# Mixture of experts on one core: the second expert's rows are transposed two blocks later, the rows' keys computed on VectorE, multiplications one stage later

## The chip, the cores and the metric

The kernel runs on one core of one Trainium2 chip. The metric is the device time of one execution in microseconds; the lower it is, the better. PE is TensorE, DVE VectorE, ACT ScalarE, POOL GpSimd and SP SyncE, whose queue issues the weight loads.

## What is computed

Two layers on 256 tokens of 1024 numbers in float32: a gated delta rule with a dense feed-forward, then attention in a window with a mixture of 8 experts, of which each token takes 2. The change is in the mixture alone:

```python
def swiglu(x, w_gate, w_up, w_down):
    return (jax.nn.silu(x @ w_gate) * (x @ w_up)) @ w_down

def moe_swiglu(x, w_router, w_gate, w_up, w_down):
    ...
    logits = (xf @ w_router).astype(jnp.float32)
    top_val, top_idx = lax.top_k(logits, TOP_K)          # TOP_K = 2
    top_w = jax.nn.softmax(top_val, axis=-1)
    gates = jnp.einsum('nk,nke->ne', top_w, jax.nn.one_hot(top_idx, N_EXPERTS, dtype=jnp.float32))
    out = jnp.zeros_like(xf)
    for e in range(N_EXPERTS):                           # 8
        h = jax.nn.silu(xf @ w_gate[e]) * (xf @ w_up[e]) # 1024 -> 3584
        out = out + gates[:, e:e + 1].astype(xf.dtype) * (h @ w_down[e])
    return out.reshape(bsz, t, d)
```

## The kernel before, in words

The mixture takes the time from about 470 us to the end. Its weights come as 336 loads of 1 MB on SP's queue into a ring of 10 buffers (`unit`, L140). Each loaded unit is split into a high and a low half: ScalarE casts `hi` (L154), VectorE subtracts to get `lo` (L155), into 4 pairs of buffers. Products of full precision are built from those halves: `mm3` (L167) takes high by high, low by high and high by low, 24 matmuls for one unit pair; a lighter form (`mm2`, L1192) packs the high and low half of up to 64 rows into one operand and takes 16. A branch on PE (`arms`, L1174) picks the form by the expert's number of rows. Expert 0 has no branch and takes the first form.

An expert's 3584 hidden numbers are 7 blocks of 512, worked through as pairs (0,1), (2,3), (4,5) and (6). The list `stages` (L1286) fixes the order of one pair: gate of both blocks, up of both blocks, the down projections of the pair before, and then "held", where the products of silu(gate) and up are multiplied (`V.tensor_mul`, L1355). The products are transposed on PE one stage later (`turn_one`, `turned`, L1240: transposes L1243, `hT` cast on ScalarE L1246, its low half on VectorE L1247). A stage is the order in the code; the scheduler sets the final order on each engine, and `issue_after` holds instructions back until the instruction that it names.

The tokens of expert 0 are picked by a one-hot matmul (L1127). Those of the other experts go through memory. `places` (L1064) works out, for each token and each of its two choices, the row in the buffer `xs`, on GpSimd with VectorE's sums between, and the two gate values `gat2`; the rows' keys become integers in `keyi` (L1079). Four scatters on GpSimd's queue (L1168, `xs<-x,keyi`) write the tokens there, each behind the landing of the one before. `fetch(e + 1)` (L1117) reads an expert's 128 rows back as `xr`, also on GpSimd's queue. `gather(e + 1)` (L1121) transposes them on PE (8 transposes, L1139), and ScalarE (L1141) and VectorE (L1142) make the halves `xg` of them, and the packed form `xp`. In the code, `fetch` is called at the up block 1 and `gather` at the up block 3 of the expert before.

Of the kernel before, what the change touches and what calls it, by code (L numbers as in the profile page):

```python
# [23 lines left out]
F32 = mybir.dt.float32  # L24
# [3 lines left out]
OP = mybir.AluOpType  # L28
AX = mybir.AxisListType

P = 128
# [7 lines left out]
E = 8  # L39
NE = 8  # L40
# [42 lines left out]
def kernel(ctx: ExitStack, tc: tile.TileContext, A, out):  # L83
# [83 lines left out]
    def mm3(ps, xh, xl, whs, first, last):  # L167
        n = len(whs)
        for k, (wh, _) in enumerate(whs):
            PE.matmul(ps, xh(k), wh, start=first and k == 0, stop=False)  # L170
            PE.matmul(ps, xl(k), wh, start=False, stop=False)  # L171
        for k, (_, wl) in enumerate(whs):
            PE.matmul(ps, xh(k), wl, start=False, stop=last and k == n - 1)  # L173
# [391 lines left out]
    p = trb()  # L565
# [498 lines left out]
    def places():  # L1064

        sq = [P, 2, E]
        row, spill, one, val = (rt.tile(sq, F32, name=n) for n in ("row", "spill", "one", "val"))
        G.tensor_tensor(row, pos, place[:, None, :E].to_broadcast(sq), op=OP.add)
        G.tensor_tensor(spill, place[:, E:, None].to_broadcast(sq), row, op=OP.subtract)
        G.tensor_scalar(val, pos, float(P), None, op0=OP.is_ge)  # L1070
        G.tensor_tensor(spill, spill, val, op=OP.mult)
        G.tensor_tensor(row, row, spill, op=OP.add)
        key = rt.tile([P, 2, 2], F32, name="key")
        for j in range(2):
            G.tensor_scalar(one, rank, float(j), None, op0=OP.is_equal)
            for src, dst in ((row, key), (gate, gat2)):
                G.tensor_tensor(val, one, src, op=OP.mult)
                V.tensor_reduce(dst[:, j], val, axis=AX.X, op=OP.add)
        V.tensor_copy(keyi, key)  # L1079
# [4 lines left out]
    with ExitStack() as mctx:  # L1084
# [36 lines left out]
        def gather(e):  # L1121
# [7 lines left out]

            if e == 0:  # L1130
                for k in range(KC):
                    pick(k, 0)
            for g in range(2):
                p = pg[g] if e == 0 else trb()
                for k in range(4 * g, 4 * g + 4):
                    if e == 0:
                        pick(k, 1)
                    else:
                        PE.transpose(p[:, k % 4 * P:(k % 4 + 1) * P], xr[e][:, k * P:(k + 1) * P], ident)  # L1139
                hi, lo = (xg[:, n, 4 * g:4 * g + 4, :].rearrange("p a c -> p (a c)") for n in range(2))  # L1140
                S.copy(hi, p)  # L1141
                V.tensor_sub(lo, p, hi.bitcast(F32))  # L1142
                if e:
                    packed(xp[e][:, 512 * g:512 * (g + 1)], p, lo)
# [17 lines left out]
        with tc.issue_after(placed.ins):  # L1162
            for tb in range(2):
                gates(tb, lgs[tb])
            places()
# [3 lines left out]
        for tb in range(2):  # L1169
            nc.gpsimd.dma_start(x3d[tb * P:(tb + 1) * P], x[tb])  # L1170
        NB = EF // 512
# [144 lines left out]

        for what, e, b in stages:
# [7 lines left out]
            if what == "gate":  # L1325
# [3 lines left out]
                if held:  # L1329
                    turn_one()  # L1330
# [5 lines left out]
            elif what == "up":  # L1336
# [5 lines left out]
                if whole:  # L1342
                    for n, (pg, pu) in enumerate(zip(pgs, pus)):
                        s_ = mp.tile([P, 512], F32, name="msg", tag="msg")
                        S.activation(s_, pg, AF.Silu)
                        mine.append((b - len(pgs) + 1 + n, pu, low(pu) if e else None, s_))
                if b == 1 and e + 1 < NE:
                    fetch(e + 1)
                if b == 3 and e + 1 < NE:
                    xg[e + 1] = gather(e + 1)  # L1350
            elif what == "held":
                if e:
                    arms(e, lambda: None, lambda: [addlow(pu, lu_) for _, pu, lu_, _ in mine])
                for bb, pu, _, s_ in mine:
                    V.tensor_mul(s_, s_, pu)  # L1355
                    held.append((e, bb, s_))
                mine.clear()
# [130 lines left out]
```

## Time and profile before

| | us |
| --- | --- |
| median of 3 runs | 1424.33 (1423.22 to 1425.75) |
| profiled execution | 1427.08 |
| its span, first to last instruction | 1425.4 |
| PE busy | 1314.1 |
| VectorE busy | 1165.6 |
| ScalarE busy | 1012.1 |
| GpSimd busy | 68.0 |

Busy times are shares of one execution that passes through stages with different limits, so they don't tell what bounds a given stage. An engine's timeline lists its instructions in order of their start; the difference between two starts is what one instruction takes of the engine, while the duration printed for a matmul holds the end of its pipeline as well. In brackets stands how long the engine was idle ahead of the instruction, and which event ended that.

### The profile page before, as it was taken

To read this page: it belongs to the slowest core of one execution; us is meant where nothing else is said; L and a number is where in the kernel's file an instruction comes from. 1 tells how busy PE (TensorE), PEld (TensorE's weight loads), DVE (VectorE), ACT (ScalarE), POOL (GpSimd) and SP (SyncE) were. 2 spreads that over 40 slices of the span, in tenths; PEclk is the share of its full clock that TensorE was granted. 3 is DMA by queue.
4 is the path that set the end of the run, shared out by engine and by line. 5 is a ranking of instruction groups with operands and counts; after the bars stand their busy time and mean duration, and the time that the engine had idled before them with its cause. 6 is when DMAs were issued, how large, how long until landed. Compare 5 with 4: busy or idle time off the path is not lost. (4 is left out here: it accounts for less than half of the span.)

```text
span 1425.4 us, 17392 instructions
## 1 busy us (share of the span) xinstructions
PE 1314.1 (92%) x6175; PEld 1046.2 (73%) x6175; DVE 1165.6 (82%) x1293; ACT 1012.1 (71%) x1264; POOL 68.0 (5%) x97
## 2 busy tenths in 40 slices
PE   7999999999898969988899999999889999888884
PEld 5888788888777858866677777776667777666663
DVE  4885975554878768889998887889999888999998
ACT  4764544443364657689888878779988888998983
POOL 4000000000000310000000000000000000002110
PEclk9999999999999889999999999999999999999997
DMA  8641577653644899999999999999999999999992
GB/s 283 208 125 60 178 271 237 229 207 120 226 148 170 307 366 336 362 368 392 419 413 380 367 358 368 376 343 408 413 420 411 377 369 374 396 414 416 419 416 87
DMA packets 145378, 446.76 MB, mean 313 GB/s; under 512 B 12704, under 2 KB 20032, under 8 KB 145264
## 3 DMA queue, kind: packets, MB, share of 16 engines
q1 hardware_dynamic: 137072, 420.64, 77.8%
q0 software_dynamic: 5280, 18.66, 3.5%
q10 hardware_dynamic: 2912, 5.90, 1.2%
q8 instruction: 76, 1.25, 0.3%
q14 instruction: 38, 0.31, 0.1%
HBM read 435.05 MB, written 15.36 MB: 316 GB/s over the span
## 5 line engine op out<-in xcount | busy, mean ns | idle before, releaser
L155 DVE TENSOR_TENSOR lo<-raw,hi 128x2048 fp32r<-128x2048 f32 (+1 forms) x610 | 910.3, 1532 | 119.1 <-ACT hi L154 109.2
L154 ACT CAST hi<-raw 128x2048 fp32r<-128x2048 f32 (+1 forms) x610 | 768.4, 1310 | 156.5 <-PE acc L171 61.3
L1195 PE MATMUL acc<-lo,xp 128*128 128x512 f32 x224 | 76.8, 431 | 22.3 <-DVE lo L155 20.1
L170 PE MATMUL acc<-hi,hT 128*128 128x512 f32 x224 | 89.1, 398 | 2.0 <-ACT hi L154 2.0
L170 PE MATMUL mm<-hi,xg 128*128 128x512 f32 x224 | 87.8, 393 | 0.5 <-ACT low L1189 0.5
L170 PE MATMUL acc<-hi,xg 128*128 128x512 f32 x224 | 87.8, 392 | 0.0
L171 PE MATMUL acc<-hi,hT 128*128 128x512 f32 x224 | 87.8, 392 | 0.0
L171 PE MATMUL mm<-hi,xg 128*128 128x512 f32 x224 | 87.4, 390 | 0.0
L171 PE MATMUL acc<-hi,xg 128*128 128x512 f32 x224 | 87.2, 389 | 0.0
L1195 PE MATMUL mm<-lo,xp 128*128 128x512 f32 x224 | 70.8, 403 | 9.6 <-DVE lo L155 9.4
L1195 PEld LDWEIGHTS acc<-lo,xp 128*128 128x128 f32 x224 | 39.6, 195 | 50.4 <-DVE lo L155 44.5
L1195 PE MATMUL acc<-lo,hp 128*128 128x512 f32 x224 | 71.5, 400 | 3.4 <-DVE lo L155 3.4
L1195 PE MATMUL acc<-hi,hp 128*128 128x512 f32 x224 | 70.8, 397 | 1.2 <-ACT hp L1115 1.2
L1195 PE MATMUL mm<-hi,xp 128*128 128x512 f32 x224 | 68.9, 394 | 2.2 <-ACT low L1189 1.5
L1195 PE MATMUL acc<-hi,xp 128*128 128x512 f32 x224 | 70.7, 403 | 0.0
L173 PE MATMUL acc<-lo,hT 128*128 128x512 f32 x224 | 69.4, 391 | 0.0
L173 PE MATMUL mm<-lo,xg 128*128 128x512 f32 x224 | 67.7, 389 | 0.0
L173 PE MATMUL acc<-lo,xg 128*128 128x512 f32 x224 | 67.7, 389 | 0.0
L1355 DVE TENSOR_TENSOR msg<-msg,acc 128x512 f32<-128x512 f32 x56 | 36.4, 681 | 36.5 <-PEq L1179 33.3
L1195 PEld LDWEIGHTS mm<-lo,xp 128*128 128x128 f32 x224 | 40.2, 188 | 26.8 <-DVE lo L155 19.4
L1114 ACT CAST hp<-tr 128x256 fp32r<-128x256 f32 x49 | 18.6, 380 | 54.7 <-DVE hT L1247 54.7
L1243 PE MATMUL tr<-ident,msg 128*128 128x128 f32 x224 | 34.9, 284 | 22.5 <-DVE msg L1355 22.5
(411 smaller groups left out, 2326.3 us busy)
## 6 DMA issues: line engine op xcount, KB each, us to landing
raw<-in_moe_w_gate_dram SPq DMA_DIRECT2D x112, 1024.0 KB, 7.6
raw<-in_moe_w_up_dram SPq DMA_DIRECT2D x112, 1024.0 KB, 7.5
raw<-in_moe_w_down_dram SPq DMA_DIRECT2D x112, 1024.0 KB, 7.9
raw<-in_a_w_in_dram SPq DMA_DIRECT2D x12, 1024.0 KB, 5.3
raw<-in_ffn_w_gate_dram SPq DMA_DIRECT2D x11, 1024.0 KB, 5.1
raw<-in_ffn_w_up_dram SPq DMA_DIRECT2D x11, 1024.0 KB, 5.0
raw<-in_ffn_w_down_dram SPq DMA_DIRECT2D x11, 1024.0 KB, 4.9
raw<-in_b_w_in_dram SPq DMA_DIRECT2D x5, 1024.0 KB, 5.0
```

What stands on the lines that cost most here:

```text
L154: S.copy(hi[:, c], raw[:, c])
L155: subs.append(V.tensor_sub(lo[:, c], raw[:, c], hi[:, c].bitcast(F32)))
L170: PE.matmul(ps, xh(k), wh, start=first and k == 0, stop=False)
L171: PE.matmul(ps, xl(k), wh, start=False, stop=False)
L173: PE.matmul(ps, xh(k), wl, start=False, stop=last and k == n - 1)
L1114: S.copy(v[:, :, 0], p)
L1195: PE.matmul(ps, x[:, (k0 + i % n) * P:(k0 + i % n + 1) * P], w, start=first and i == 0, stop=last and i == 2 * n - 1)
L1243: PE.transpose(p[:, f * P:(f + 1) * P], s[:, f * P:(f + 1) * P], ident)
L1355: V.tensor_mul(s_, s_, pu)
```

## The change

It has three parts. `gather(1)`, for expert 1 alone, is called at the up block 5 in place of 3, and its transposes are held back behind the last matmul that `mm3` has recorded by then (`turn[0]`); the other experts' gathers stay at block 3. `places` computes the keys on VectorE (four instructions, then three for each of the two choices, each choice with its own cast to `keyi`) and runs ahead of `gates`; the gate values move to `pair_gates`, on GpSimd with VectorE's sums, behind the scatters. The multiplications move from "held" to behind the gate of the next pair's first block, and the transposes of the products with them by one stage; those of the pair (4,5) and of the very last block stay in "held".

```diff
@@ -170,7 +170,7 @@
             PE.matmul(ps, xh(k), wh, start=first and k == 0, stop=False)
             PE.matmul(ps, xl(k), wh, start=False, stop=False)
         for k, (_, wl) in enumerate(whs):
-            PE.matmul(ps, xh(k), wl, start=False, stop=last and k == n - 1)
+            turn[0] = PE.matmul(ps, xh(k), wl, start=False, stop=last and k == n - 1)
 
     def mm3_steps(ps, xh, xl, whs, first, last):
         n = len(whs)
@@ -1064,19 +1064,23 @@
     def places():
 
         sq = [P, 2, E]
-        row, spill, one, val = (rt.tile(sq, F32, name=n) for n in ("row", "spill", "one", "val"))
-        G.tensor_tensor(row, pos, place[:, None, :E].to_broadcast(sq), op=OP.add)
-        G.tensor_tensor(spill, place[:, E:, None].to_broadcast(sq), row, op=OP.subtract)
-        G.tensor_scalar(val, pos, float(P), None, op0=OP.is_ge)
-        G.tensor_tensor(spill, spill, val, op=OP.mult)
-        G.tensor_tensor(row, row, spill, op=OP.add)
+        row, spill, val = (rt.tile(sq, F32, name=n) for n in ("row", "spill", "val"))
         key = rt.tile([P, 2, 2], F32, name="key")
+        V.tensor_tensor(row, pos, place[:, None, :E].to_broadcast(sq), op=OP.add)
+        V.tensor_tensor(spill, place[:, E:, None].to_broadcast(sq), row, op=OP.subtract)
+        V.scalar_tensor_tensor(spill, pos, float(P), spill, op0=OP.is_ge, op1=OP.mult)
+        V.tensor_add(row, row, spill)
         for j in range(2):
-            G.tensor_scalar(one, rank, float(j), None, op0=OP.is_equal)
-            for src, dst in ((row, key), (gate, gat2)):
-                G.tensor_tensor(val, one, src, op=OP.mult)
-                V.tensor_reduce(dst[:, j], val, axis=AX.X, op=OP.add)
-        V.tensor_copy(keyi, key)
+            V.scalar_tensor_tensor(val, rank, float(j), row, op0=OP.is_equal, op1=OP.mult)
+            V.tensor_reduce(key[:, j], val, axis=AX.X, op=OP.add)
+            V.tensor_copy(keyi[:, j], key[:, j])
+
+    def pair_gates():
+        val = rt.tile([P, 2, E], F32, name="gval")
+        for j in range(2):
+            G.tensor_scalar(val, rank, float(j), None, op0=OP.is_equal)
+            G.tensor_tensor(val, val, gate, op=OP.mult)
+            V.tensor_reduce(gat2[:, j], val, axis=AX.X, op=OP.add)
 
     def at(j, tb):
         return bass.IndirectOffsetOnAxis(ap=keyi[:, j, tb:tb + 1], axis=0)
@@ -1127,16 +1131,20 @@
                 PE.matmul(pg[k // 4][:, (k % 4) * P:(k % 4 + 1) * P], x[tb][:, k * P:(k + 1) * P], Pe[e][:, tb, :],
                           start=tb == 0 and k % 4 == 0, stop=tb == 1 and k % 4 == 3)
 
+            late = ExitStack()
             if e == 0:
                 for k in range(KC):
                     pick(k, 0)
+            elif e == 1:
+                late.enter_context(tc.issue_after(turn[0].ins))
             for g in range(2):
                 p = pg[g] if e == 0 else trb()
-                for k in range(4 * g, 4 * g + 4):
-                    if e == 0:
-                        pick(k, 1)
-                    else:
-                        PE.transpose(p[:, k % 4 * P:(k % 4 + 1) * P], xr[e][:, k * P:(k + 1) * P], ident)
+                with late.pop_all():
+                    for k in range(4 * g, 4 * g + 4):
+                        if e == 0:
+                            pick(k, 1)
+                        else:
+                            PE.transpose(p[:, k % 4 * P:(k % 4 + 1) * P], xr[e][:, k * P:(k + 1) * P], ident)
                 hi, lo = (xg[:, n, 4 * g:4 * g + 4, :].rearrange("p a c -> p (a c)") for n in range(2))
                 S.copy(hi, p)
                 V.tensor_sub(lo, p, hi.bitcast(F32))
@@ -1160,14 +1168,16 @@
         G.memset(fold.bitcast(F32), 0.0)
         S.copy(fold[:, :HALF], ident[:, HALF:])
         with tc.issue_after(placed.ins):
-            for tb in range(2):
-                gates(tb, lgs[tb])
             places()
         for j in range(2):
             for tb in range(2):
                 nc.gpsimd.indirect_dma_start(out=xs[:, :], out_offset=at(j, tb), in_=x[tb][:, :], in_offset=None)
         for tb in range(2):
             nc.gpsimd.dma_start(x3d[tb * P:(tb + 1) * P], x[tb])
+        with tc.issue_after(placed.ins):
+            for tb in range(2):
+                gates(tb, lgs[tb])
+            pair_gates()
         NB = EF // 512
         acc, flags = {}, {}
         y = []
@@ -1314,6 +1324,12 @@
             e, b, s = held.pop(0)
             hT[e, b] = turned(s, e)
 
+        def multiply():
+            for bb, pu, _, s_, ee in mine:
+                V.tensor_mul(s_, s_, pu)
+                held.append((ee, bb, s_))
+            mine.clear()
+
         for what, e, b in stages:
             if what != "held":
                 nxt = next(nexts, None)
@@ -1326,7 +1342,9 @@
                 if b % 2 == 0:
                     pgs = [mm() for _ in range(1 if whole else 2)]
                 gateup(e, b, us, pgs)
-                if held:
+                if b % 2 == 0 and b < NB - 1:
+                    multiply()
+                elif held:
                     turn_one()
                 if whole:
                     lgs_ = [low(p) if e else None for p in pgs]
@@ -1343,18 +1361,16 @@
                     for n, (pg, pu) in enumerate(zip(pgs, pus)):
                         s_ = mp.tile([P, 512], F32, name="msg", tag="msg")
                         S.activation(s_, pg, AF.Silu)
-                        mine.append((b - len(pgs) + 1 + n, pu, low(pu) if e else None, s_))
+                        mine.append((b - len(pgs) + 1 + n, pu, low(pu) if e else None, s_, e))
                 if b == 1 and e + 1 < NE:
                     fetch(e + 1)
-                if b == 3 and e + 1 < NE:
+                if b == 5 - 2 * (e > 0) and e + 1 < NE:
                     xg[e + 1] = gather(e + 1)
             elif what == "held":
                 if e:
-                    arms(e, lambda: None, lambda: [addlow(pu, lu_) for _, pu, lu_, _ in mine])
-                for bb, pu, _, s_ in mine:
-                    V.tensor_mul(s_, s_, pu)
-                    held.append((e, bb, s_))
-                mine.clear()
+                    arms(e, lambda: None, lambda: [addlow(pu, lu_) for _, pu, lu_, _, _ in mine])
+                if b == NB - 2 or (e, b) == (NE - 1, NB - 1):
+                    multiply()
                 if (e, b) == (NE - 1, NB - 1):
                     turn_one()
                 if (e, b) == (NE - 2, NB - 1):
```

PE, expert 0, around the transposes of expert 1's rows (`xr`), before. `xg_4205` are expert 0's tokens, so the row ahead is the end of an up block; `hT` is an operand of a down block.

```order
L170 MATMUL acc_4616<-hi_4611,xg_4205 128x512
L171 MATMUL acc_4616<-hi_4611,xg_4205 128x512
L173 MATMUL acc_4616<-lo_4612,xg_4205 128x512 x2
L1139 MATMUL tr_4683<-ident_73,xr_4509 128x128 x4
L1139 MATMUL tr_4692<-ident_73,xr_4509 128x128 x4
L170 MATMUL acc_4725<-hi_4643,hT_4556 128x512
```

And now:

```order
L170 MATMUL acc_4876<-hi_4871,xg_4205 128x512
L171 MATMUL acc_4876<-hi_4871,xg_4205 128x512
L173 MATMUL acc_4876<-lo_4872,xg_4205 128x512 x2
L1147 MATMUL tr_4951<-ident_73,xr_4509 128x128 x4
L1147 MATMUL tr_4960<-ident_73,xr_4509 128x128 x4
L170 MATMUL acc_4705<-hi_4911,hT_4860 128x512
```

They stood between the up blocks of the second pair and the down blocks of the first; now they stand between the up blocks of the third pair and the down blocks of the second, 144 matmuls and 8 transposes of products later.

VectorE at the start of expert 0, the end of the key and gate instructions, before. The two `xg<-acc` subtractions of expert 0 stand nine rows ahead of the first row here.

```order
L1042 TENSOR_SCALAR gate<-gate,gden_4245 128x8
L1041 RECIPROCAL gden_4254<-gden_4254 128x1
L155 TENSOR_TENSOR lo<-raw,hi 128x512
L1042 TENSOR_SCALAR gate<-gate,gden_4254 128x8
L155 TENSOR_TENSOR lo<-raw,hi 128x512
L1078 TENSOR_REDUCE gat_4194<-val 128x2
L155 TENSOR_TENSOR lo<-raw,hi 128x512
L1078 TENSOR_REDUCE key<-val 128x2
L155 TENSOR_TENSOR lo<-raw,hi 128x512
L1078 TENSOR_REDUCE gat_4194<-val 128x2
L1079 CAST keyi<-key 128x4
```

And now, with the first of those subtractions as the last row:

```order
L1074 SCALAR_TENSOR_TENSOR val<-rank,row 128x16
L1038 TENSOR_TENSOR gate<-gate,sel 128x8 x2
L1075 TENSOR_REDUCE key<-val 128x2
L1040 TENSOR_REDUCE gden_4265<-gate 128x1
L1040 TENSOR_REDUCE gden_4274<-gate 128x1
L1076 CAST keyi<-key 128x2
L1074 SCALAR_TENSOR_TENSOR val<-rank,row 128x16
L1041 RECIPROCAL gden_4265<-gden_4265 128x1
L1041 RECIPROCAL gden_4274<-gden_4274 128x1
L1075 TENSOR_REDUCE key<-val 128x2
L1042 TENSOR_SCALAR gate<-gate,gden_4265 128x8
L1150 TENSOR_TENSOR xg<-acc,xg 128x512
```

The first `keyi` stood behind both subtractions and five quarters of a weight's split (`lo`); now it stands ahead of the first subtraction, and its second half twelve rows further on. Of the quarters, two stood ahead of the subtractions that now stand behind them.

GpSimd, from the last key instructions to the fetch of `xr`, before:

```order
L1077 TENSOR_TENSOR val<-one,gate 128x16
L1075 TENSOR_SCALAR one<-rank 128x16
L1077 TENSOR_TENSOR val<-one,row 128x16
L1077 TENSOR_TENSOR val<-one,gate 128x16
L1168 DMA xs<-x_75,keyi 1280x1024
L1168 DMA xs<-x_76,keyi 1280x1024
L1168 DMA xs<-x_75,keyi 1280x1024
L1168 DMA xs<-x_76,keyi 1280x1024
L1119 DMA xr<-xs 128x1024 x2
```

And now:

```order
L1081 TENSOR_SCALAR gval<-rank 128x16
L1174 DMA xs<-x_75,keyi 1280x1024
L1082 TENSOR_TENSOR gval<-gval,gate 128x16
L1081 TENSOR_SCALAR gval<-rank 128x16
L1082 TENSOR_TENSOR gval<-gval,gate 128x16
L1174 DMA xs<-x_76,keyi 1280x1024
L1174 DMA xs<-x_75,keyi 1280x1024
L1174 DMA xs<-x_76,keyi 1280x1024
L1123 DMA xr<-xs 128x1024 x2
```

Of the key and gate instructions three gate ones are left between the first scatter and the second, and one ahead of the first; eleven stood ahead of it.

On SP's queue the loads stand in the same order. In expert 1, the eight transposes of expert 2's rows stood four ahead of the first up block and four behind it, and are now one piece ahead of it. From there on PE, VectorE and ScalarE have the same instructions in the same order before and after, the multiplications and their transposes too.

## Rows read from the trace of the kernel before

**Rows 1.** The head of the page: the span and the instructions of the program, then each engine's busy time, its share of the span and its instructions.

```profile
span 1425.4 us, 17392 instructions
...
PE 1314.1 (92%) x6175; PEld 1046.2 (73%) x6175; DVE 1165.6 (82%) x1293; ACT 1012.1 (71%) x1264; POOL 68.0 (5%) x97
```

**Rows 2.** The table of waits from 430 us to the end: engine, tile and line, what was waited for, us in total, times, longest us (PEq is PE's sequencer).

```profile
DVE msg L1355 <- PEq L1179: 33.3, 12, 3.8
...
PE tr L1243 <- DVE msg L1355: 22.5, 27, 1.1
...
PE tr L1139 <- DMA xr<-xs: 10.8, 1, 10.8
...
DVE lo L155 <- DMA raw<-in_moe_w_gate_dram: 5.9, 4, 1.6
```

**Rows 3.** The PE timeline around the down blocks of expert 0's first pair: start, us, operation, count, and in brackets the idle time before it and who ended it.

```profile
497.14 0.39 PE L170 MATMUL mm<-hi,xg 128*128 128x512 f32 x1
...
502.58 0.60 PE L1243 MATMUL tr<-ident,msg 128*128 128x128 f32 x4
502.94 0.47 PE L170 MATMUL mm<-hi,xg 128*128 128x512 f32 x1
...
519.43 0.61 PE L173 MATMUL acc<-lo,xg 128*128 128x512 f32 x2
530.82 1.94 PE L1139 MATMUL tr<-ident,xr 128*128 128x128 f32 x8 [10.78 <-DMA xr<-xs]
532.40 0.78 PE L170 MATMUL acc<-hi,hT 128*128 128x512 f32 x1
...
534.26 1.05 PE L173 MATMUL acc<-lo,hT 128*128 128x512 f32 x2
...
535.38 0.40 PE L171 MATMUL acc<-hi,hT 128*128 128x512 f32 x1
```

**Rows 4.** Stretches of 20 us on core 0: busy time and instructions of PE, its weight loads, VectorE, ScalarE and GpSimd, the granted clock of PE as a share of its full speed, the mean busy share of the DMA engines, GB/s.

```profile
500.00:520.00 20.00, 20.00 (x93) 16.23 (x91) 18.11 (x12) 15.62 (x15) 4.85 (x2) 1.00 1.02 418
520.00:540.00 20.00, 9.22 (x37) 7.77 (x37) 7.98 (x14) 7.25 (x16) 1.15 (x2) 0.74 0.72 279
540.00:560.00 20.00, 20.00 (x94) 16.53 (x93) 17.10 (x13) 15.64 (x14) 0.00 (x0) 1.00 0.96 346
560.00:580.00 20.00, 20.00 (x90) 16.57 (x89) 17.79 (x11) 14.38 (x8) 0.00 (x0) 1.00 0.99 373
580.00:600.00 20.00, 20.00 (x94) 16.55 (x93) 17.73 (x10) 14.87 (x11) 0.00 (x0) 1.00 0.98 357
...
1340.00:1360.00 20.00, 17.03 (x72) 12.08 (x71) 19.30 (x13) 17.42 (x18) 0.00 (x0) 1.00 1.02 420
```

**Rows 5.** The VectorE timeline at the start of expert 0, and behind the transposes of `xr` (columns as in rows 3).

```profile
472.96 0.17 DVE L1078 TENSOR_REDUCE key<-val 128x2 f32<-128x16 f32 x1 [0.73 <-POOL val L1077]
473.05 0.68 DVE L155 TENSOR_TENSOR lo<-raw,hi 128x512 fp32r<-128x512 f32 x1
473.65 0.23 DVE L1038 TENSOR_TENSOR gate<-gate,sel 128x8 f32<-128x8 f32 x2
473.80 0.68 DVE L155 TENSOR_TENSOR lo<-raw,hi 128x512 fp32r<-128x512 f32 x1
474.94 0.69 DVE L1142 TENSOR_TENSOR xg<-acc,xg 128x512 fp32r<-128x512 f32 x1 [0.46 <-ACT xg L1141]
...
481.24 14.53 DVE L155 TENSOR_TENSOR lo<-raw,hi 128x512 fp32r<-128x512 f32 x24
...
532.56 0.69 DVE L1142 TENSOR_TENSOR xg<-tr,xg 128x512 fp32r<-128x512 f32 x1 [11.13 <-ACT xg L1141]
```

**Rows 6.** The GpSimd timeline: the four scatters of the rows and the issue of `xr` behind them.

```profile
481.63 1.29 POOL L1168 DMA_INDIRECT xs<-x,keyi  x1 [0.58 <-DVE keyi L1079]
488.98 7.65 POOL L1168 DMA_INDIRECT xs<-x,keyi  x1 [6.06 <-DMA xs<-x,keyi]
504.52 2.87 POOL L1168 DMA_INDIRECT xs<-x,keyi  x1 [7.89 <-DMA xs<-x,keyi]
514.55 1.98 POOL L1168 DMA_INDIRECT xs<-x,keyi  x1 [7.16 <-DMA xs<-x,keyi]
523.85 0.59 POOL L1119 DMA_DIRECT2D xr<-xs  x1 [7.31 <-issue]
```

**Rows 7.** The PE timeline in expert 1, around the transposes of expert 2's rows.

```profile
636.82 0.60 PE L1139 MATMUL tr<-ident,xr 128*128 128x128 f32 x4
...
638.69 0.74 PE L1195 MATMUL acc<-lo,xp 128*128 128x512 f32 x2 [0.80 <-DVE lo L155]
...
641.06 0.74 PE L1195 MATMUL acc<-lo,xp 128*128 128x512 f32 x2 [0.24 <-DVE lo L155]
...
643.86 0.74 PE L1195 MATMUL acc<-lo,xp 128*128 128x512 f32 x2 [0.21 <-DVE lo L155]
...
647.19 0.73 PE L1195 MATMUL acc<-lo,xp 128*128 128x512 f32 x2 [1.19 <-DVE lo L155]
```

**Rows 8.** The ScalarE timeline in the same stretch: the cast that reads the second bank of transposes last.

```profile
641.79 0.42 ACT L1114 CAST hp<-tr 128x256 fp32r<-128x256 f32 x1
```

**Rows 9.** The PE timeline where expert 1 begins.

```profile
615.96 0.50 PE L170 MATMUL acc<-hi,hT 128*128 128x512 f32 x1 [1.99 <-ACT hi L154]
...
616.91 0.88 PE L1195 MATMUL acc<-lo,xp 128*128 128x512 f32 x2
...
620.78 0.62 PE L1195 MATMUL acc<-hi,xp 128*128 128x512 f32 x2
```

**Rows 10.** The waits of SP's queue (the weight loads) from 520 to 610 us.

```profile
SPq L145 <- DVE lo L155: 75.0, 26, 15.2
```

## The prediction

> **What bounds the kernel now.** I read the page first: PE is busy 1314.1 of 1425.4 us, VectorE 1165.6, ScalarE 1012.1 [rows 1]. On average PE is the limit, but an average doesn't price a change in one place, so the table of waits over the mixture of experts came next. There PE stands once, for 10.8 us, in front of the transposes of `xr` (L1139), until the DMA that brings expert 1's rows has landed [rows 2]; no other single PE wait of that table is near it. The PE timeline shows what stands around it [rows 3]: the matmuls follow each other without a gap up to 519.43, the transposes begin at 530.82, and the matmuls behind them run slower at first. The windows tell whether PE is the limit on both sides of that hole [rows 4]: 20.00 of 20 us in 500 to 520 and in each of the three windows from 540 to 600, 9.22 in 520 to 540. So here every microsecond taken out of PE's hole should come out of the whole, unless something else is late next. The profiled execution took 1427.08 us with a span of 1425.4; the median of the runs is 1424.33, 2.75 us less. I make the sum as a difference and take it off the median.
>
> **The hole (gather of expert 1 two blocks later).** One matmul of expert 0 costs 0.2267 us: 24 of them lie between 497.14 and 502.58 [rows 3]. The last pair at 519.43 is therefore done at 519.88. The hole is 530.82 - 519.88 = 10.94 us. The eight transposes then take 532.40 - 530.82 = 1.58 us, where four took 502.94 - 502.58 = 0.36 elsewhere, so eight should take 0.72: 0.86 us too much. The seven matmuls from 532.40 to 535.38 take 2.98 us, where 7 x 0.2267 = 1.59 are due: 1.39 too much. The granted clock of that window is 0.74 [rows 4], and PE had stood still just before it fell: part of the time is spent at the lower of the two levels, 1.2 GHz in place of 2.4. All three go if the transposes find their rows: 10.94 + 0.86 + 1.39 = **13.2 us**. The transposes themselves stay, 0.72 us, at the new place, which is no change.
>
> Do they find them? In PE's order 144 matmuls and eight transposes of products now lie between the old place and the new: 48 down, 48 gate, 48 up. Without the hole, PE comes to them at 519.88 + 144 x 0.2267 + 0.72 = 553.2, on the clock of the old trace. There the rows land at 530.8. Even if the scatters start no earlier, 22.4 us are left.
>
> **What is late next.** VectorE stood idle for 11.13 us behind the same transposes, ahead of 532.56 [rows 5], so it loses its wait with PE. Its rate with PE full is known: 17.10 to 17.79 of 20 us in the three windows behind the hole [rows 4]; it keeps up. ScalarE has 14.38 to 15.64 there. For the loads see rival C.
>
> **Keys on VectorE.** `places` was three VectorE instructions between GpSimd ones; now it is ten, and they stand ahead of the first `xg` subtraction, with two quarters of a weight's split pushed behind it. I count 13 small instructions more ahead of it. In the old trace VectorE waited 0.73 us there for GpSimd's `val` and 0.46 for ScalarE's `xg`, and a quarter takes 0.60 (473.05 to 473.65): cover of 0.73 + 0.46 + 2 x 0.60 = 2.4 us. Against it stand 13 small ones; two take 0.15 from 473.65 to 473.80, so 13 take 1.0 [rows 5]. Nothing is due. If the cover fails, because ScalarE is sooner, the first gate matmuls on the low half are late by at most the length of one `xg` subtraction, 0.7 us. I take **+0.2**, bounds 0 and 0.7. What it buys, the first scatter at about 475 in place of 481.63 [rows 6], pays nothing by itself, since 22.4 us were already to spare; it adds 6 to them. The gate halves left on GpSimd are not waited for by PE here.
>
> **Multiplications one stage later.** In expert 0 the products of blocks 0 and 1 are multiplied and transposed later; the eight transposes cost the same 0.72 in either place, and PE did not wait for them before (no gap at 502.58) [rows 3]. For the other experts the order of PE, VectorE and ScalarE is the same before and after, row by row, except for one place in expert 1: I price the move there at **0**. Its waits (22.5 us of PE for products, 27 times [rows 2]) stay.
>
> **Expert 1's one new piece.** The eight transposes of expert 2's rows stood four and four around an up block; now they are one piece. The first four went at 636.82; the bank that the second four need is freed by ScalarE's `hp` cast at 641.79 + 0.42 = 642.21 [rows 7, 8]. So PE may be held from 636.82 + 0.36 = 637.18, at most 5.0 us. In the next eight microseconds PE stood waiting for VectorE anyway, 0.80 + 0.24 + 0.21 + 1.19 = 2.44 us [rows 7], and could make that up. Bounds 0 and 2.6. I take **+0.5**, near the lower end, since expert 1 runs at VectorE's pace and four split buffers let that engine go on while PE is held.
>
> **Below nothing.** The start of expert 1 has a PE wait of 1.99 us for ScalarE at 615.96, and the ten matmuls from 616.91 to 620.78 take 3.87 where 2.27 are due, 1.6 more [rows 9]. Both could come out otherwise once the engines meet 13 us earlier, though nothing in the change touches them: 0 in the sum, -3.6 in the range.
>
> Sum: -13.2 + 0.2 + 0 + 0.5 = -12.5; 1424.33 - 12.5 = **1411.8 us** (1414.6 for a profiled execution like the old one).
>
> **The rivals.**
> A, the forecast: 1411.8.
>
> B, the multiplications' move works for all experts after all, and PE's 22.5 us of waits for products go as well: 1411.8 - 22.5 = 1389.3. Against it: the order, which shows the same rows there. It would also show that the change does more than its order says. 3 in 100.
>
> C, the weight loads take the gain back. The DMA engines' busy share in the windows behind the hole is 0.96 to 0.99 [rows 4], which looks full; then PE would wait for weights instead and the time stays near 1424. Against it: those windows move 346 to 373 GB/s, while 1340 to 1360 moves 420 [rows 4], so there is room; SP's queue waits 75.0 us between 520 and 610 for VectorE to free a load buffer [rows 10], so loads wait for the consumer; and VectorE waits for a gate weight only 5.9 us in the whole stretch [rows 2]. The last two experts do run near the highest rate, but their loads are tied to the buffers freed before them, which come 12 us sooner too. 6 in 100, mostly in part.
>
> D, slower: the rows come late again at the new place. The four scatters are issued by GpSimd one after the other, each behind the landing of the one before; issue spans are 1.29, 7.65, 2.87 and 1.98 us, the long one while VectorE ran 14.53 us of subtractions without a break from 481.24 [rows 5, 6]. With VectorE busier at the new start more of them could be long. From the first scatter to the rows is 49.2 us (481.63 to 530.82). Up to 22.4 us more costs nothing; since a new hole would bring the 0.86 + 1.39 = 2.25 us of slow clock again, the kernel is slower from 22.4 + 12.5 - 2.25 = 32.7 us more. At twice the length the rows land at 580.0, PE waits 26.8 us and pays those 2.25: 1424.33 - 12.5 + 26.8 + 2.25 = 1440.9. Against it: it needs almost a doubling. 2 in 100.
>
> On D the Trainium skill has a rule, in "SBUF — State Buffer", section "Who interferes with whom": GpSimd writes the descriptors of a DMA on its own queue through a port that it shares with VectorE, and an instruction that holds the port locks the other out, though a subtraction with both inputs in SBUF is said to take only the port's read side. The 7.65 us row speaks rather for a lock of some kind beside such subtractions; no row here separates the two. If it held for all four issues, the rows would come 4 x 7.65 - 13.79 = 16.8 us later, at 547.6, and that is still ahead of 553.2: the sum stays as it is.
>
> **How the numbers follow.** A 0.89, B 0.03, C 0.06, D 0.02. A's own range: the upper bounds give -13.2 + 0.7 + 2.6 = -9.9, 1414.4, and runs lie up to 1.4 above their median: 1416. The lower: -13.2 - 3.6 = -16.8, 1407.5. This leaves out B, D and most of C, 1 in 10, and the bounds of A are themselves none too sure, so I leave it there. About 0.2% (2.8 us) is what a measurement can tell from no change. Faster by more: A, B and part of C, 0.93. Within: the rest of C, 0.05. Slower: D, 0.02.
>
> **What would show it.** In the profile after: no PE wait at the transposes of `xr` in expert 0, PE at 20 of 20 us and a clock of 1.00 from 500 to 580; the rows landed some 25 us before PE uses them; expert 1's first gate block 13 us earlier; the waits of VectorE's products on PE's sequencer the same 12 times and about 33 us; 13 us earlier all along to the end. Wrong would be: a wait of PE for weights between 540 and 600 (C), a scatter chain over 70 us (D), the products' waits gone (B), or a stretch after expert 1 in which the 13 us melt, which I have no term for.

## The result and the profile after

The changed kernel's median is 1414.68 us (1412.96 to 1418.36, 5 runs) beside 1424.33 (1422.67 to 1427.30, 5 runs) before: a ratio of 0.9938 with a 95% interval of 0.9918 to 0.9959, or 9.65 us less. The forecast was 1411.8, with a range of 1407.5 to 1416.0. The profiled execution took 1412.96 us.

The head of the page of the kernel after, which answers to [rows 1]: PE's busy time fell 4.7 us and the span 14.1, so most of what went was idle time.

```profile
span 1411.3 us, 17398 instructions
...
PE 1309.4 (93%) x6175; PEld 1042.5 (74%) x6175; DVE 1165.8 (83%) x1300; ACT 1013.4 (72%) x1264; POOL 67.3 (5%) x90
```

The table of waits of the kernel after from 430 us to the end (columns as in [rows 2]). The wait of PE for the DMA of `xr`, 10.8 us, is gone. The products' two waits stand where they stood, 33.1 for 33.3 and 22.6 for 22.5, with the same counts.

```profile
DVE msg L1329 <- PEq L1189: 33.1, 12, 3.8
...
PE tr L1253 <- DVE msg L1329: 22.6, 27, 1.1
...
PE tr L1147 <- ACT hp L1118: 3.8, 3, 2.3
```

The PE timeline of the kernel after at four places: the old and the new place of the transposes of `xr` [rows 3], the start of expert 1 [rows 9], and expert 1 around the transposes of expert 2's rows [rows 7].

```profile
519.50 0.62 PE L173 MATMUL acc<-lo,xg 128*128 128x512 f32 x2
519.95 0.39 PE L170 MATMUL acc<-hi,hT 128*128 128x512 f32 x1
...
553.11 0.62 PE L173 MATMUL acc<-lo,xg 128*128 128x512 f32 x2
553.56 1.03 PE L1147 MATMUL tr<-ident,xr 128*128 128x128 f32 x8
554.35 0.47 PE L170 MATMUL acc<-hi,hT 128*128 128x512 f32 x1
...
602.99 0.51 PE L170 MATMUL acc<-hi,hT 128*128 128x512 f32 x1 [1.99 <-ACT hi L154]
...
606.23 0.62 PE L1205 MATMUL acc<-hi,xp 128*128 128x512 f32 x2
...
622.31 0.60 PE L1147 MATMUL tr<-ident,xr 128*128 128x128 f32 x4
625.20 0.66 PE L1147 MATMUL tr<-ident,xr 128*128 128x128 f32 x4 [2.29 <-ACT hp L1118]
...
626.63 1.05 PE L1205 MATMUL acc<-hi,xp 128*128 128x512 f32 x2
```

No hole is left behind 519.50; the eight transposes at 553.56 (forecast 553.2) wait for nothing and take 0.79 us. Expert 1 begins at 602.99 in place of 615.96, 12.97 us sooner, and behind its slow first matmuls PE is at 606.23 where it was at 620.78: 14.55 sooner. At the end of the span it is 14.1. The one piece for expert 2's rows is held 2.29 us, and behind it some matmuls run slower: the pair at 626.63 is busy 1.05 us, the one at 606.23 0.62.

The windows of the kernel after (columns as in [rows 4]). PE is full in the four shown of expert 0, at a clock of 1.00, while the loads now run at 386 to 420 GB/s, near the 420 that [rows 4] shows at 1340. The last window shown, below full clock at 0.91, lies in expert 1, around the hold of the one piece.

```profile
500.00:520.00 20.00, 20.00 (x94) 16.55 (x93) 18.37 (x13) 15.65 (x15) 1.88 (x2) 1.00 1.03 420
520.00:540.00 20.00, 20.00 (x90) 16.57 (x89) 18.34 (x20) 15.21 (x17) 0.00 (x0) 1.00 1.03 417
540.00:560.00 20.00, 20.00 (x98) 16.61 (x97) 18.24 (x14) 16.21 (x18) 0.58 (x1) 1.00 1.04 417
560.00:580.00 20.00, 20.00 (x94) 16.54 (x93) 18.29 (x10) 15.13 (x12) 0.00 (x0) 1.00 1.01 386
620.00:640.00 20.00, 17.49 (x71) 13.17 (x69) 18.60 (x12) 20.00 (x25) 0.60 (x2) 0.91 1.01 391
```

GpSimd's timeline of the kernel after answers to [rows 6]. The first scatter starts 7.4 us sooner, but the third issue is 12.11 us long, so `xr` is issued 8.1 us sooner, at 515.71. From the issue to the landing passed 7.1 us, so the rows lay there at 522.8, 30.8 us ahead of their use.

```profile
474.25 1.12 POOL L1174 DMA_INDIRECT xs<-x,keyi  x1 [3.93 <-DVE key L1075]
...
479.32 1.27 POOL L1174 DMA_INDIRECT xs<-x,keyi  x1 [0.47 <-issue]
487.44 12.11 POOL L1174 DMA_INDIRECT xs<-x,keyi  x1 [6.84 <-DMA xs<-x,keyi]
506.19 1.29 POOL L1174 DMA_INDIRECT xs<-x,keyi  x1 [6.64 <-DMA xs<-x,keyi]
515.71 0.59 POOL L1123 DMA_DIRECT2D xr<-xs  x1 [8.22 <-issue]
```

VectorE's timeline of the kernel after [rows 5]: the first `xg` subtraction starts at 475.03, where it started at 474.94, so the keys were covered; then comes one run of 30 quarters, 19.74 us, where there were 24 and 14.53.

```profile
475.03 0.69 DVE L1150 TENSOR_TENSOR xg<-acc,xg 128x512 fp32r<-128x512 f32 x1 [0.66 <-ACT xg L1149]
...
478.97 19.74 DVE L155 TENSOR_TENSOR lo<-raw,hi 128x512 fp32r<-128x512 f32 x30
498.63 0.69 DVE L1329 TENSOR_TENSOR msg<-msg,acc 128x512 f32<-128x512 f32 x1
```

### The profile page after: what moved, and what is told of

Read it like the earlier page. It is cut to its first block, busy times and chain, and to the rows that moved or that the text cites. A ratio compares the mean times of both kernels' runs of the same rounds, so it can differ in the third digit from the quotient of the medians.

```text
span 1411.3 us, 17398 instructions
## 1 busy us (share of the span) xinstructions
PE 1309.4 (93%) x6175; PEld 1042.5 (74%) x6175; DVE 1165.8 (83%) x1300; ACT 1013.4 (72%) x1264; POOL 67.3 (5%) x90
## 5 line engine op out<-in xcount | busy, mean ns | idle before, releaser
L1329 DVE TENSOR_TENSOR msg<-msg,acc 128x512 f32<-128x512 f32 x56 | 36.5, 684 | 36.0 <-PEq L1189 33.1
L1253 PE MATMUL tr<-ident,msg 128*128 128x128 f32 x224 | 34.9, 284 | 22.6 <-DVE msg L1329 22.6
```

The source lines that it names most:

```text
L1253: PE.transpose(p[:, f * P:(f + 1) * P], s[:, f * P:(f + 1) * P], ident)
```

## The experiments

**1. The gather's move alone, from the kernel before.**

```diff
-                if b == 3 and e + 1 < NE:
+                if b == 5 - 2 * (e > 0) and e + 1 < NE:
```

(with the `late` lines in `gather`)

> The kernel before with the first part alone: expert 1's rows transposed two blocks later, keys and multiplications as before. My theory (the whole gain is the hole at these transposes, and the rows were in time at the new place anyway): no PE wait at the transposes, the rows landed about 22 us ahead of their use, 12 to 14 us less than before, as much as the whole change. Rival (the earlier keys are needed for it): a wait of some microseconds remains and less than 10 us is gained.

Measured: 1413.35 us (6 runs) beside 1424.94 (17), ratio 0.9911 (0.9892 to 0.9931). In its PE timeline the transposes wait for nothing:

```profile
555.48 0.62 PE L173 MATMUL acc<-lo,xg 128*128 128x512 f32 x2
555.94 1.03 PE L1143 MATMUL tr<-ident,xr 128*128 128x128 f32 x8
```

The late read by itself gives the whole gain, 11.6 us between the medians (12 to 14 expected).

**2. The keys alone, from the kernel before.**

```diff
         with tc.issue_after(placed.ins):
-            for tb in range(2):
-                gates(tb, lgs[tb])
             places()
...
+        with tc.issue_after(placed.ins):
+            for tb in range(2):
+                gates(tb, lgs[tb])
+            pair_gates()
```

(with `places` on VectorE, as in the change)

> The kernel before with the second part alone: keys on VectorE ahead of the gates, rows still transposed at the old place. The rows land 7.9 us earlier in the changed kernel (522.8 in place of 530.7), PE wants them at 519.9. My theory: the hole shrinks from 10.9 to about 3 us, and if so short a pause leaves the clock alone, the 2.25 us of slow clock go too: 8 to 10 us less than before. Rival (the keys bring nothing unless the gather moves): within 2 us of before.

Measured: 1414.52 us (6), ratio 0.9922 (0.9903 to 0.9941). PE timeline at the old place, and GpSimd's:

```profile
520.41 0.61 PE L173 MATMUL acc<-lo,xg 128*128 128x512 f32 x2
521.59 1.07 PE L1143 MATMUL tr<-ident,xr 128*128 128x128 f32 x8 [0.57 <-DMA xr<-xs]
522.41 0.47 PE L170 MATMUL acc<-hi,hT 128*128 128x512 f32 x1
```

```profile
488.33 9.94 POOL L1170 DMA_INDIRECT xs<-x,keyi  x1 [6.81 <-DMA xs<-x,keyi]
...
514.53 0.59 POOL L1123 DMA_DIRECT2D xr<-xs  x1 [8.46 <-issue]
```

The sooner scatters shrink the wait to 0.57 us, and the transposes behind it take 0.82, with no slow stretch. So this part alone gives the whole gain as well: the two are substitutes. It does so with nothing to spare; the change has 30.8 us. The one piece for expert 2's rows is there too, held 2.57 us at 627.15, and not in experiment 1, so it comes with the earlier keys.

**3. The multiplications alone, from the kernel before.**

```diff
-                if held:
+                if b % 2 == 0 and b < NB - 1:
+                    multiply()
+                elif held:
                     turn_one()
```

(with `multiply` and the end of "held", as in the change)

> The kernel before with the third part alone: multiplications and the products' transposes one stage later. My theory (only expert 0 is reordered, where PE didn't wait for the products): the hole of 10.8 us stays, and the time is within 1.5 us of before. Rival B of the prediction: PE's 22.5 us of waits for products go, and the kernel is about 10 to 22 us faster.

Measured: 1427.13 us (12), ratio 1.0013 (0.9998 to 1.0029). The hole is still there; by the prediction's working it is 529.82 - 522.78 = 7.04 us, with 0.87 too much in the transposes and 1.65 in the eight matmuls behind them:

```profile
522.33 0.61 PE L173 MATMUL acc<-lo,xg 128*128 128x512 f32 x2
529.82 1.94 PE L1139 MATMUL tr<-ident,xr 128*128 128x128 f32 x8 [6.87 <-DMA xr<-xs]
```

**4. The change without the multiplications** (parts 1 and 2 above together, nothing else).

> The change without its third part: late gather and early keys, multiplications as before. My theory (the third part does nothing): the time of the changed kernel, 1412 to 1416. Rival (the third part costs or gives something in expert 0): more than 3 us to either side.

Measured: 1414.69 us (6) beside 1424.86 (17), ratio 0.9942 (0.9921 to 0.9963): the change. Expert 2's rows are held in one piece here too, 2.52 us at 626.57, as the change's are.

**5. Five scatters more, from the kernel after.** They write rows again that are already there, so the output stays; the chain gets longer by a known number of links (rival D).

```diff
+        for _ in range(5):
+            nc.gpsimd.indirect_dma_start(out=xs[:, :], out_offset=at(1, 1), in_=x[1][:, :], in_offset=None)
```

> The changed kernel with five more scatters (the last one repeated, which writes the same rows again), each behind the landing of the one before. The rows landed at 522.8 us in the changed kernel and PE took them at 553.6; from the third scatter's end to the issue of the read some 9.5 us pass per scatter. My theory (only lateness beyond 30.8 us costs, and it costs its full length on PE): the rows land 5 x 9.5 = 47.5 us later, near 570; a hole of about 17 us is back at the transposes, with about 2 us of slow clock behind it, and the run takes about 1431 to 1434. Rival (a late read hides elsewhere, or the gain came from the order on PE and not from the rows): within 3 us of the changed kernel.

Measured: one run, 1429.58 us, below the 1431 to 1434 expected. `xr` is issued at 559.87 where the first of the five was issued at 515.68, 44.2 / 5 = 8.84 us a link where 9.5 were reckoned. PE timeline:

```profile
553.73 0.61 PE L173 MATMUL acc<-lo,xg 128*128 128x512 f32 x2
566.83 1.94 PE L1147 MATMUL tr<-ident,xr 128*128 128x128 f32 x8 [12.48 <-DMA xr<-xs]
568.42 0.77 PE L170 MATMUL acc<-hi,hT 128*128 128x512 f32 x1
...
571.01 0.40 PE L170 MATMUL acc<-hi,hT 128*128 128x512 f32 x1
```

From 554.18, when the pair at 553.73 is done, to 566.83 are 12.65 us; the transposes take 1.59 in place of 0.72, the six matmuls behind them 2.59 in place of 1.36: 12.65 + 0.87 + 1.23 = 14.75. The time rose by 14.90 over the change's median; for a single run, with the change's own runs 5.4 us apart, so near an agreement is luck. Over the change's profiled run it rose by 16.62: 0.62 lie ahead of the hole (553.73 against 553.11), and at the start of expert 1 the slow matmuls of [rows 9] are back, twelve in 4.46 us from 618.55 to 623.01 where the change has 2.86 from 603.37 to 606.23, 1.60 more. What is left, 14.4, is the hole: it costs its length and those 2.1 us, and next to nothing of it is made up later.

**6. The kernel before, profiled a second time.** The kernel is unchanged.

> The kernel before, once more, for its profile alone. The profiled run of the prediction took 1427.08 us with a hole of 10.8 us, 2.75 above the median. My theory of the size: the hole differs from run to run with the landing of the scatters, and the one shown was on the long side; another profile shows 6 to 10 us. Rival: the hole is the same within 1 us and the difference lies elsewhere (the clock, the layers ahead).

Measured: 1422.97 us, PE timeline:

```profile
518.58 0.61 PE L173 MATMUL acc<-lo,xg 128*128 128x512 f32 x2
526.81 1.94 PE L1139 MATMUL tr<-ident,xr 128*128 128x128 f32 x8 [7.61 <-DMA xr<-xs]
528.40 0.77 PE L170 MATMUL acc<-hi,hT 128*128 128x512 f32 x1
...
530.99 0.40 PE L170 MATMUL acc<-hi,hT 128*128 128x512 f32 x1
```

By the prediction's working: 526.81 - 519.03 = 7.78, and 0.87 and 1.23 more, 9.88 us, where the first profile gave 13.2. Of the 4.11 us between the two profiled runs (1427.08 and 1422.97) the hole is 3.3, and 0.85 lie ahead of it (519.43 against 518.58).

**7. The products' transposes inside the branch, from the kernel after.** The 22.6 us that the change left: each product's transposes are issued at the end of both arms of a gate or up block, and the multiplications go back to the stage of before.

```diff
+                post()
...
+        def turning(e):
+            if not e or not held:
+                return None, lambda: None
+            p, s = trb(), held[0][2]
+            return p, lambda: flip(p, s)
...
-                gateup(e, b, us, pgs)
+                pt, post = turning(e)
+                gateup(e, b, us, pgs, post=post)
```

> Late gather and keys as in the change, multiplications as before, but for experts 1 to 7 the transposes of a product are written inside both arms of the branch of the next pair's gate blocks, behind the matmuls, so that they can't be put ahead of them. It does what the third part was to do. My theory: the ten or so PE waits of 0.94 us for products in the experts with three matmuls go, 9 us less than the changed kernel, about 1405; those of the light experts (0.69 each) are covered by VectorE and bring little. Rival: the wait is only handed on (ScalarE and VectorE read the transposes later, PE waits for the down operands instead), and the time is that of the changed kernel, about 1414.

Measured: 1442.54 us (5) beside 1424.94, ratio 1.0119 (1.0100 to 1.0139); 27.9 us above the change. Its waits from 430 to 1440 us: PE waits for products 1.2 us in place of 22.6, but for the banks of the rows' transposes 20.1 in place of 3.8. These two nearly cancel. VectorE's low halves and ScalarE's `hp` make PE wait more (27.5 for 20.8, 11.9 for 1.2), and around the gathers the granted clock falls: six of the ten bank waits are 2.75 us long, at 627.7, 744.3, 873.6, 996.7, 1113.2 and 1236.1, and each of the 20 us windows that hold them is at 0.83 to 0.91, as the one below. The kernel after has 1.00 in all of these but the first. How the 27.9 us divide between waits and clock was not measured further.

```profile
PE acc L1205 <- DVE lo L155: 27.5, 30, 2.6
...
PE tr L1147 <- ACT hp L1118: 20.1, 10, 2.7
...
PE tr L1254 <- DVE msg L1379: 1.2, 1, 1.2
```

```profile
860.00:880.00 20.00, 15.69 (x66) 12.15 (x65) 16.05 (x11) 15.60 (x21) 0.53 (x1) 0.91 0.84 306
```

**8. The same, with the rows' transposes in the arms of up block 3.**

```diff
+                if e and b == 3 and e + 1 < NE:
+                    pr = [trb(), trb()]
+                    post = lambda: rows_into(e + 1, pr)
```

> The last kernel again (products transposed inside both arms of the branch), but the transposes of the next expert's rows are inside the arms too, behind up block 3. The last one lost 2.5 to 3.4 us twice at each gather, since the rows' transposes came while both transposing banks still held products. My theory: that loss goes and the waits of 0.94 us stay away, so 5 to 10 us less than the changed kernel, about 1405 to 1409. Rival (the bank conflict was only part of it: PE now waits at the branches' ends or for operands made later): not faster than the changed kernel, 1414 or more.

Measured: 1422.71 us (12) beside 1424.86, ratio 0.9992 (0.9976 to 1.0007); 8.0 us above the change. My theory, that the bank was the only price, fell. In its waits both are gone, but PE waits 38.7 us for VectorE's low halves, where the kernel after has 20.8, and 12.7 for ScalarE's `hp`. My reading, which no run tests by itself: the products' waits were mostly not PE's to lose, since in these experts VectorE and ScalarE set the pace, and a wait of PE taken away comes back at the next thing that they make.

```profile
PE acc L1209 <- DVE lo L155: 38.7, 43, 2.6
...
PE acc L1209 <- ACT hp L1119: 12.7, 8, 2.1
```

**9. Breaks in VectorE's run, from the kernel before.** A small memset behind every fourth quarter of a split asks whether the run holds GpSimd's long issue. The tile for it is 32 bytes a partition.

```diff
+                if gap[0] is not None and nq == 4 and q == 3:
+                    with tc.issue_after(subs[-1].ins):
+                        subs[-1] = V.memset(gap[0], 0.0)
...
+    gap[0] = rt.tile([P, 8], F32, name="gap")
```

> The kernel before, with one small memset of 128 x 8 on VectorE behind every fourth quarter of a split in expert 0 (behind each unit that is split in quarters), nothing else. In all six profiles of a kernel so far one scatter's issue is long (7.65 to 12.1 us), and it ends 0.65 to 0.92 us after the first multiplication starts that follows VectorE's unbroken run of 24 to 30 such quarters. Theory (the run of subtractions with both inputs in SBUF holds GpSimd's issue up until another kind of instruction comes): the long issue shrinks to 1 to 3 us, the rows land some 5 us earlier, the hole shrinks from 7 to 11 us to 2 to 6, and the time is about 5 us less than before. Rival (the issue is long because of the queue or the scatter itself, and the run's end only falls together with it): the long issue stays at 7 us or more and the time is that of before within 1.5 us.

Measured: 1428.19 us (12) beside 1424.70 (17), ratio 1.0018 (1.0006 to 1.0031): slower, though the wait of PE fell to 1.60 us. GpSimd's second issue took 1.03 us (7.65 in [rows 6]). But in the experts that run three matmuls a weight, expert 0 among them, PE was slower; the last rows are from a later one:

```profile
488.08 1.03 POOL L1173 DMA_INDIRECT xs<-x,keyi  x1 [6.09 <-DMA xs<-x,keyi]
```

```profile
521.78 1.06 PE L1144 MATMUL tr<-ident,xr 128*128 128x128 f32 x8 [1.60 <-DMA xr<-xs]
...
771.27 0.40 PE L174 MATMUL mm<-hi,xg 128*128 128x512 f32 x1
...
772.67 0.40 PE L174 MATMUL mm<-hi,xg 128*128 128x512 f32 x1
```

Six matmuls take 1.40 us, 0.2333 each, with no gap and at full clock (1.00 from 760 to 780).

**10. Breaks and keys together.** Edits 2 and 9.

> The same memsets on top of early keys (second part of the change alone). Its long issue took 9.94 us. Theory: it shrinks to 1 to 3 us and the read of the rows is issued 7 to 9 us earlier, near 506 in place of 514.5; PE's 0.57 us in front of the transposes go and nothing else, so the time is that of the early keys alone, 1412 to 1417. Rival: it stays near 10.

Measured: one run, 1426.91 us, where 1412 to 1417 were expected. The long issue is 0.95 us (9.94 with the keys alone), `xr` is issued at 503.83 and its transposes wait for nothing; what that should have given is lost in the same slower matmuls.

**11. The tile at 64 bytes.** The question is whether a 32-byte step of the tiles behind it slows the matmuls.

```diff
-    gap[0] = rt.tile([P, 8], F32, name="gap")
+    gap[0] = rt.tile([P, 16], F32, name="gap")
```

> The kernel with the memsets again, its small tile 64 bytes per partition in place of 32; nothing else differs. In the last two runs the long issue went (7.65 to 1.03 and 9.94 to 0.95 us) and the hole shrank to 1.6 us and to nothing, but the 10 us gained at 560 us melted to 1 us by 1213: the matmuls of the experts with three products took 0.232 and 0.235 us each in place of 0.2267. The 32 bytes had moved all tiles allocated behind it, the operands xg and hT among them, from a multiple of 64 bytes to 32 beyond one. Theory (the addresses cost it): 0.2267 us per matmul again, the 10 us stay, 1413 to 1417, about 10 less than before. Rival (the memsets themselves or the order cost it): the matmuls stay at 0.232 and more, the time within 3 us of before.

Measured: 1428.12 us (12) beside 1423.96 (16), ratio 1.0024 (1.0009 to 1.0039): no better; six matmuls from 770.40 to 771.80 again take 1.40. That a multiple of 64 bytes is enough fell.

**12. The memset into a tile that is there and no longer read**, so that no address moves.

```diff
-    gap[0] = rt.tile([P, 16], F32, name="gap")
+    gap[0] = before[:, 0, :]
```

> The kernel with the memsets once more, written into a tile that is no longer used (before), so that no tile is added and every address is that of the kernel before. With the added tile of 64 bytes the matmuls of the experts with three products took 0.2305 and 0.236 us, so a multiple of 64 bytes doesn't help, and the theory in that form has fallen. Theory (the shifted addresses cost it, at a coarser step than 64 bytes): the matmuls take 0.2267 again, the 8 to 10 us gained by the shorter issue stay, 1413 to 1417. Rival (the memsets or what they change in the order cost it, not the addresses): 0.23 us and more per matmul, the time at or above that of before, 1424 to 1429.

Measured: 1417.57 us (6) beside 1424.62 (11), ratio 0.9951 (0.9935 to 0.9967). The expected 1413 to 1417 is missed by 0.6. GpSimd's issue is short, a wait of 1.78 us is left ahead of the transposes, and PE's six matmuls take 1.36 us again:

```profile
490.25 1.16 POOL L1173 DMA_INDIRECT xs<-x,keyi  x1 [5.97 <-DMA xs<-x,keyi]
```

```profile
520.74 0.61 PE L177 MATMUL acc<-lo,xg 128*128 128x512 f32 x2
523.14 1.06 PE L1144 MATMUL tr<-ident,xr 128*128 128x128 f32 x8 [1.78 <-DMA xr<-xs]
...
771.65 0.39 PE L174 MATMUL mm<-hi,xg 128*128 128x512 f32 x1
...
773.01 0.39 PE L174 MATMUL mm<-hi,xg 128*128 128x512 f32 x1
```

So breaks alone give 7 us as a third substitute, with a hole of 523.14 - 521.19 = 1.95 us left. PE, ScalarE and GpSimd run the same instructions in the same order as in experiment 9, and VectorE's differ in the places of two memsets; what is left as the cause of the slower matmuls is where the tiles lie, and the moved addresses had cost 1428.19 - 1417.57 = 10.6.

## Why the prediction was right, and where a size was off

**The hole** was the right step, and the price of its own profile was right too: 13.2 us forecast, 12.97 at 602.99. The term was mis-sized for the median. The scatters' landing varies from run to run: the working gives 13.2 in the first profile, 9.9 in the second (experiment 6) and 9.6 in experiment 3 (7.04 + 0.87 + 1.65). I took one profile's hole, the longest of the three, off the median, and the forecast of 1411.8 is 2.9 us too low. The profiled run of before lay 2.75 us above its median, that of after 1.72 below its: of the 14.12 between the two, 9.65 are left between the medians, close to the second profile's 9.88. That the median run's hole is as short as that is not measured, and not all of a run's distance from the median is its hole: the change's runs lie 5.4 us apart without one.

**What is late next**: nothing in expert 0. VectorE runs 18.24 to 18.37 of 20 us and PE is full. **Rival C** is refuted by the windows: the loads rose to 417 GB/s instead of holding PE.

**Keys, +0.2**: did not show; 475.03 against 474.94. (`places` had five instructions on VectorE before, not three; nothing of the sum hangs on it.) That the sooner scatter "pays nothing by itself" is right beside the gather's move only. Alone it pays everything (experiment 2), which the sentence didn't say.

**Multiplications, 0**: held. Their waits stayed to 0.2 us, alone they give nothing that can be measured (experiment 3), and without them the change is the same (experiment 4). **Rival B** fell; and experiments 7 and 8 put its price in doubt as well: with those 22.6 us of waits taken away by the branch's arms the kernel is 8.0 us or more slower than the change.

**One piece, +0.5**: the hold was there, 2.29 us (at most 5.0 forecast), and behind it slower matmuls, for which the prediction had no term. Neither cost anything lasting, since VectorE's waits made them up, as forecast: PE was 14.55 us sooner ahead of the hold, at 606.23, and 14.57 at the end of the block (639.56 in place of 654.13); at the end of the span it was 14.1.

**Below nothing**: of the two at the start of expert 1, the wait of 1.99 stayed and the slow matmuls went, 14.55 - 12.97 = 1.6 us, in the profiled run, which took 1412.96 where 1414.6 was forecast for it. The hole doesn't decide that: the twelve matmuls behind the wait take 4.44 us before (616.34 to 620.78), 4.44 in experiment 1, which has no hole (605.73 to 610.17), 2.87 in experiment 2 and 2.86 in the change. What does decide it is open.

**Rival D** had the right price and too little behind it: the third issue took 12.11 us, longer than any before, but 30.8 us were to spare; in the one run that used them up the lateness beyond them was paid in full (experiment 5). The reckoning behind it put the rows at 547.6 if all four issues were held; one was, and they came at 522.8.

## What to carry to other kernels

When PE waits for a late transfer, reading it later and starting it sooner are substitutes: price each alone, since the second one buys slack, not time. The length of such a wait varies from run to run, so take it from more than one profile before it comes off a median. A profiled run's total doesn't tell how long the wait was: that of experiment 3 took 1427.49 us with a hole of 7.04, the first one 1427.08 with 10.94. A wait of PE in a stretch where another engine sets the pace need not be PE's to gain, and a new small tile can move the addresses of everything behind it.

## What the hardware showed that I had not expected

**A run of VectorE holds one scatter's issue.** The long issue ends just behind the run's end: 496.63 against 481.24 + 14.53 = 495.77 before [rows 5, 6], 499.55 against 498.71 after. A run that ends later gives a longer issue (7.65, 9.94 in experiment 2, 12.11), and breaks shrink it to 1.03 and 1.16 (experiments 9 and 12). Open is why the first scatter at 481.63 was issued in 1.29 us [rows 6], and the change's second at 479.32 in 1.27, though both lie inside the run, within 0.4 us of its start; and whether what is held is the reading of the offsets or the writing of the descriptors. The Trainium skill, "SBUF — State Buffer", section "Who interferes with whom", says that a VectorE instruction with two SBUF inputs contends with what GpSimd reads, and infers that such a subtraction doesn't stall the writing of descriptors. The trace agrees with a contention: an issue is held by such subtractions. Whether the inference on the descriptors holds no run here shows, since the parts of an issue are not told apart.

**Matmuls depend on where their operands lie.** Shifting the tiles by 32 or 64 bytes took 0.2267 us a matmul to 0.2333 (1.36 to 1.40 for six), with the same work (experiments 9, 11 and 12). In the four experts of three matmuls (expert 0 and three later ones), 42 weight loads of 12 matmuls each, that is an estimated 4 x 42 x 12 x 0.0067 = 13.5 us, more than the 10.6 measured; the 0.0067 comes from two stretches of six, read to 0.01 us. Start to start the traces of experiments 9 and 11 give 0.233 in each of the four, where the expectations of 11 and 12 have 0.2305 to 0.236. Which operand's place matters and which step would be harmless are open.

**The price of a hole beside its length** didn't grow with it: 2.5 us for 7.04, 2.1 for 7.78, 2.25 for 10.94 and 2.1 for 12.65 (experiments 3 and 6, the first profile, experiment 5), with a granted clock of 0.73 to 0.83 in the 20 us windows around them. Behind pauses of 0.57 and 1.78 there was none, at 1.00 (experiments 2 and 12). The pause's length alone doesn't tell: behind the same wait of 1.99 us at the start of expert 1 matmuls ran slower before and not in the change.
